# Conditioning in four column groups, norms three steps later, gate rows and y loaded ahead, merged tokens split as they are merged

## The chip, the cores and the metric

One core of one Trainium2 chip. The metric is device time in microseconds (us). Engines are named as the profile names them: PE (TensorE matmul), PEld (its weight loads), DVE (VectorE), ACT (ScalarE), POOL (GpSimd), SP (SyncE, which issues all the DMAs named here).

## The reference

One layer over 1024 sample tokens (a 16x64 grid) and 128 prompt tokens, together NT = 1152 columns, with D = 1024:

```
shift, scale, gate = split(silu(cond) @ w_ada + b_ada, 3)
h = rmsnorm(x, norm_g) * (1 + scale) + shift
q, k, v, z_a, u_b, z_b, u_c, z_c, g_a, g_b, g_c = split(h @ w_in)
q, k = rmsnorm per head (64 wide) of q, k
y_a = neighbourhood attention (8 x 16 window, bias) + cached context keys
y_b = Fourier mixing of u_b;  y_c = pooling of u_c
merged = sum over i of sigmoid(g_i) * ((silu(z_i) * y_i) @ p_i)
out = x + gate * (merged @ w_o);   new k and v of the prompt are returned
```

## The kernel before

Nearly every large product is three matmuls of high and low halves (hi·hi, lo·hi, hi·lo; `mm3`, L143 to L146), in fp16 up to the gates and in a rounded fp32 form in the last projection. The program is written in one order; a list scheduler then fixes, before the run, the order of each engine's instructions, and each engine runs its own list strictly in order. A wait at the head of an engine's list therefore holds all that is behind it. [...]

**Conditioning** (0 to 63 us). SP loads 16 pieces of 512 KB of `w_ada` (`wa`, six buffers) and nine tiles of x (`xt`, six buffers). `ada_piece` (L355) multiplies the silu of the two conditioning rows, two columns wide, with a piece in fp32: two matmuls of 512 columns a piece, each recorded twice in the trace (64 records). `ada_end` (L364) copies a finished bank (ACT, `ar`), transposes it on PE and adds the bias on DVE. Meanwhile `xnorms` (L324) squares three tiles of x on ACT, takes the root on POOL and scales on DVE; `x_groups` (L341) transposes them on PE and copies them back by ACT (L350). `h_full` (L407) applies scale and shift, `scale_h` (L380) bounds h, `make_h` (L414) makes its halves. The weight of head pair 0 is squared (L74, `wjk_q`), scaled and split (L98, `wh_q`; L99, `wl_q`).

**Head pairs** (63 to 400 us). A pair's q, k, v come as nine token tiles of 8 steps of `mm3` (`p1_tiles`, L284). `p1_evac` (L247) squares on ACT, sums on DVE, and takes the root and the row of factors on POOL (`rs` L255, `rg` L257). `p1_norm` (L267) multiplies the PSUM tile by `rg` on DVE (`tk`, L271) and splits it into halves (`tok`, L279); it stands after step k == 3 of the next tile. `group_q` (L565) and `group_k` (L581) transpose four normed tiles on PE; `new_pair` makes the pair's factors (`grow`, L232). `chain()` (L757) lays these on steps with `at_(step, ...)`, and 312 steps of it are dealt out between the items of attention (scores, exp, transposes `pt` -> `pts` L686, products `po` L702), after a first fill of 32 + 9 steps.

**Branches and gate rows** (400 to 535 us). Pooling (C) and Fourier (B), then 16 groups of `p_products` (`pec`, `peb` written to DRAM). After every second one a 512 KB piece of the gate weight is loaded (`wg`, L1126 to L1154) and added up on DVE (`acc`, L1144, L1146); four matmuls (`gb`, L1151) sum it over partitions at the end.

**Attention's gates** (535 to 640 us). For four blocks, y is loaded (`ya`, L1195), the product z_a is made (`za`), gated, and multiplied with p_a (`ppa`, L1248).

**Gates by Strassen's method** (640 to 889 us; `xa`, `xb`, `xc`). A finished block of the merged tokens (`mg`) is written to DRAM (`m_d`).

**Output projection** (889 to 998 us). `wo_unit` (L1382) loads and splits w_o, `m_load` and `m_split` (L1399) read the merged tokens back and split them (`mh` L1400, `ml` L1401); 18 tiles of 8 steps of `mm3` (`wo`).

## Time and profile before

| | us |
|---|---|
| three runs | 993.22, 998.97, 997.37 (median 997.37) |
| the profiled execution, its own time | 999.48 |
| its span in the trace | 997.7 |
| busy on POOL, with its share of the span | 228.5 (23%) |
| busy on ACT | 495.0 (50%) |

The span is 1.8 us short of the execution's own time. Times below are counted from the start of the span. An engine's busy share is an average over the stages just named; what a stage costs is read from what waits last in it. In lists of waits, the engine that waited stands first and behind the arrow what it waited for.

### The profile page before, as it was taken

The page shows a single profiled execution, that of the slowest core. Times are in us where ns is not written, and L with a number is a line of the kernel's source. Part 1 is how long each engine was busy: PE and PEld are TensorE (multiplying, and loading weights), DVE is VectorE, ACT ScalarE, POOL GpSimd, SP SyncE. Part 2 cuts the span into 40 slices and gives each one's busy share as a digit, 9 for nine tenths or more (in the row PEclk, how much of TensorE's full clock was granted, in tenths as well). Part 3 has the DMA queues.
Part 4 walks back from the last instruction along what each step waited for, and adds up shares of the span by engine and source line. Part 5 has one row for each costly group of instructions (what it writes and reads, how often), then busy time and mean ns, then how long its engine had stood idle before and what let it go on. Part 6 is the DMA issues. An engine that isn't in the chain of part 4 may idle for free.

```text
span 997.7 us, 17549 instructions
## 1 busy us (share of the span) xinstructions
PE 916.2 (92%) x6510; PEld 675.4 (68%) x6510; DVE 648.5 (65%) x1431; ACT 495.0 (50%) x1023; POOL 228.5 (23%) x373
## 2 busy tenths in 40 slices
PE   4976799898889999989989899999999999989998
PEld 1333466565656676657975479888888888868886
DVE  1365557667676664797543559878979788766422
ACT  4683557557556665545435434555554544433100
POOL 1056454444545320041100320002021020200000
PEclk9978989999999999999999999999999999989999
DMA  7743322312302322411878502443435332248421
GB/s 305 272 133 104 101 70 78 81 40 75 83 25 75 101 74 78 145 53 49 257 245 281 173 33 91 173 139 112 145 118 163 98 115 95 68 142 303 130 95 54
DMA packets 72038, 123.95 MB, mean 124 GB/s; under 512 B 10592, under 2 KB 39180, under 8 KB 71953
## 3 DMA queue, kind: packets, MB, share of 16 engines
q1 hardware_dynamic: 71953, 122.84, 38.6%
q8 instruction: 51, 0.84, 0.3%
q14 instruction: 34, 0.28, 0.1%
HBM read 87.41 MB, written 28.84 MB: 117 GB/s over the span
## 4 chain that ended last, share of the span: by engine, by line
PE 65%; DVE 11%; DMA 8%; POOL 7%; ACT 5%; issue 3%; SPq 1%; ACTq 0%; DVEq 0%; POOLq 0%
PE wo L144 3%; PE wo L145 3%; PE wo L146 3%; PE xc L146 3%; PE xb L144 3%; PE xb L146 3%; PE xb L145 3%; PE xc L144 3%; PE xc L145 3%; POOL rs L255 3%; PE xa L144 3%; PE xa L146 3%; PE xa L145 3%; PE ppa L144 2%; PE ppa L146 2%
## 5 line engine op out<-in xcount | busy, mean ns | idle before, releaser
L145 PE MATMUL p<-wl_q,hh 128*128 128x384 f16 x288 | 96.9, 336 | 1.0 <-DVE wl_q L99 1.0
L144 PE MATMUL p<-wh_q,hh 128*128 128x384 f16 x288 | 96.1, 337 | 0.0
L146 PE MATMUL p<-wh_q,hl 128*128 128x384 f16 x288 | 96.0, 336 | 0.0
L673 ACT ACTIVATE sn<-sn,mn 128x512 f32<-128x512 f32 x64 | 46.3, 724 | 30.6 <-DVE mn L662 29.1
L144 PE MATMUL wo<-woh,mh 128*128 128x512 f32 x144 | 57.6, 400 | 3.0 <-ACT mh L1400 3.0
L145 PE MATMUL wo<-wol,mh 128*128 128x512 f32 x144 | 56.9, 397 | 0.0
L146 PE MATMUL wo<-woh,ml 128*128 128x512 f32 x144 | 56.5, 394 | 0.0
L686 DVE TENSOR_TENSOR pts<-pt,pts 128x512 f16<-128x512 f32 (+1 forms) x72 | 46.0, 639 | 11.3 <-ACT pts L685 10.9
L88 POOL TENSOR_SCALAR wsc_g<-wsc_g 128x1 f32<-128x1 f32 x12 | 2.7, 228 | 207.0 <-DVE wsc_g L87 207.0
L271 DVE TENSOR_TENSOR tk<-p,rg 128x256 f32<-128x256 f32 x36 | 15.3, 424 | 52.6 <-POOL rg L257 52.6
L1441 DVE TENSOR_TENSOR yo<-wo,gb 128x512 f32<-128x512 f32 x18 | 12.4, 690 | 53.7 <-PE wo L146 53.7
L662 DVE CUSTOM_DVE_ANT_0 sn<-s,bias 128x512 f32<-128x512 f32 x64 | 43.6, 681 | 5.4 <-PE s L658 5.4
L702 PEld LDWEIGHTS <-pts 128*128 128x128 f16 x792 | 33.6, 98 | 16.0 <-DVE pts L686 9.2
L145 PEld LDWEIGHTS <-wh_m 128*128 128x128 f16 x288 | 28.4, 98 | 23.1 <-issue 6.5
L146 PEld LDWEIGHTS <-hl 128*128 128x128 f16 x288 | 29.0, 101 | 21.2 <-issue 3.6
L146 PEld LDWEIGHTS <-wl_m 128*128 128x128 f16 x288 | 28.4, 99 | 21.3 <-DVE wl_m L99 2.5
L702 PE MATMUL po<-vw,pts 128*128 128x64 f16 x576 | 32.6, 193 | 11.0 <-DVE pts L686 7.0
L144 PEld LDWEIGHTS <-wh_m 128*128 128x128 f16 x288 | 28.8, 100 | 18.5 <-issue 1.7
L145 PEld LDWEIGHTS <-hh 128*128 128x128 f16 x288 | 29.0, 101 | 17.8 <-issue 1.9
L144 PEld LDWEIGHTS <-hh 128*128 128x128 f16 x288 | 29.0, 101 | 17.4 <-issue 1.4
L362 PE MATMUL pa<-wa,sil 128*2 128x512 f32 x64 | 31.0, 633 | 10.1 <-DMA wa<-in_wss_dram 10.1
L685 ACT CAST pts<-pt 128x512 f16<-128x512 f32 (+1 forms) x72 | 38.9, 540 | 1.3 <-PE pt L683 1.2
(654 smaller groups left out, 3060.4 us busy)
## 6 DMA issues: line engine op xcount, KB each, us to landing
wa<-in_wss_dram SPq DMA_DIRECT2D x16, 512.0 KB, 4.3
wr_q<-in_w_dram SPq DMA_DIRECT2D x16, 384.0 KB, 3.0
wr_m<-in_w_dram SPq DMA_DIRECT2D x24, 256.0 KB, 3.0
pp_c<-pec SPq DMA_DIRECT2D x24, 192.0 KB, 2.7
pp_b<-peb SPq DMA_DIRECT2D x24, 192.0 KB
pp_a<-pea SPq DMA_DIRECT2D x24, 192.0 KB, 1.8
ppxc<-pp_c SPq DMA_DIRECT2D x16, 288.0 KB, 2.7
ppxb<-pp_b SPq DMA_DIRECT2D x16, 288.0 KB, 2.9
```

The costliest lines, as they stand in the source:

```text
L144: T.matmul(out, lh, rh, start=first, stop=False)
L145: T.matmul(out, lh, rl, start=False, stop=False)
L146: T.matmul(out, ll, rh, start=False, stop=last)
L255: G.tensor_tensor(rs, rs, mhalf, op=ALU.pow)
L271: V.tensor_tensor(tk, pt[:, :256], rg.rearrange("p g d -> p (g d)"), op=ALU.mult)
L362: T.matmul(pa[:2], sil[:, k], wa[i][:, q], start=(k == 0), stop=(k == KT - 1))
L662: V.tensor_tensor_reduce(out=sn, in0=pS, in1=bt.rearrange("p a b -> p (a b)"), op0=ALU.add, op1=ALU.min, scale=1.0, scalar=3e38, accum_out=mn)
L673: S.activation(e[:, :n], it["sn"], AF.Exp, bias=it["mn"], scale=-1.0, accum_out=sm_)
L685: S.copy(pts[:, 0, :n], pt[:, :n])
L686: V.tensor_tensor(pts[:, 1, :n], pt[:, :n], pts[:, 0, :n], op=ALU.subtract)
L702: T.matmul(po[:, :64], it["pts"][:, a, j * P:(j + 1) * P], it["vl"][j][:, c_ * 64:(c_ + 1) * 64], start=(j == 0 and i == 0), stop=(j == nk ...
L1441: V.tensor_tensor(yo, pt, gb[0 if t == 8 else 1][:, cols], op=ALU.mult)
```

## The change

It has five parts. (a) The silu rows are padded to 32 columns and these matmuls go to four column groups of PE (`tile_position`); the groups are summed by a matmul with `pick` in place of the transposes. Two `wa` pieces are loaded ahead of x, and the weight of pair 0 is squared, scaled and split ahead of the last `ada_end`. (b) Five small operations of `new_pair` go from POOL to DVE. (c) `p1_norm` stands after k == 6, and `group_q`, `group_k`, `setup_prompt` and `windows` later accordingly; the fill is 32 + 13. (d) Weights of the products and gate rows are loaded two ahead, `acc` is spread over the groups, the four `gb` stand in the last two groups, and two of the four `ya` loads stand before the end of the products. (e) Columns 0 to 511 of the merged tokens are split as they are merged and stay in SBUF (`mh0`, `ml0`); only the rest goes through `m_d`. The first three `wo_unit` stand in the last Strassen unit.

```diff
...
-    sil = pers.tile([P, KT, 2], F32, name="sil")
+    sil = pers.tile([P, KT, 32], F32, name="sil")
+    pick = pers.tile([P, 2], F32, name="pick")
...
-                    G.tensor_scalar(gs4[:, 2 * i:2 * i + 2], sc_[:, 2 * p:2 * p + 2], inv, None, op0=ALU.mult)
-                    G.tensor_tensor(g[:, 2 * i:2 * i + 2], row.unsqueeze(1).to_broadcast([P, 2, 64]),
+                    V.tensor_scalar(gs4[:, 2 * i:2 * i + 2], sc_[:, 2 * p:2 * p + 2], inv, None, op0=ALU.mult)
+                    V.tensor_tensor(g[:, 2 * i:2 * i + 2], row.unsqueeze(1).to_broadcast([P, 2, 64]),
...
-                G.tensor_scalar(i8, inv, 0.125, None, op0=ALU.mult)
+                V.tensor_scalar(i8, inv, 0.125, None, op0=ALU.mult)
...
-                        if k == 3 and late:
+                        if k == 6 and late:
...
-                V.tensor_tensor(sil.rearrange("p k c -> p c k"), ex.rearrange("p (c k) -> p c k", c=2),
+                G.memset(sil, 0.0)
+                V.tensor_tensor(sil[:, :, 0:2].rearrange("p k c -> p c k"), ex.rearrange("p (c k) -> p c k", c=2),
                                 col[:, 0:16].rearrange("p (c k) -> p c k", c=2), op=ALU.mult)
+                V.reduce_sum(pick, ident.rearrange("p (g c) -> p c g", g=4)[:, 0:2], axis=AX.X)
...
-                        T.matmul(pa[:2], sil[:, k], wa[i][:, q], start=(k == 0), stop=(k == KT - 1))
+                        g = 32 * (k % 4)
+                        T.matmul(pa[g:g + 32], sil[:, k], wa[i][:, q], start=(k < 4), stop=(k >= 4), tile_position=(0, g))
                 def ada_end(b):
-                    ar = st.tile([2, 512], F32, tag="ar", name=f"ar{b}", bufs=2)
-                    S.copy(ar, pas[b][:2, :])
+                    ar = st.tile([P, 512], F32, tag="ar", name=f"ar{b}", bufs=1)
+                    S.copy(ar, pas[b])
...
                     for j in range(4):
-                        T.transpose(pb[:, 2 * j:2 * j + 2], ar[:, j * P:(j + 1) * P], ident[:2, :2])
+                        T.matmul(pb[:, 2 * j:2 * j + 2], ar[:, j * P:(j + 1) * P], pick, start=True, stop=True)
...
-                for what in (0, 1, 2, "w0", "w1", 3, 4, 5, "w2", "w3", "w4", "w5"):
+                for what in ("w0", "w1", 0, 1, 2, "w2", "w3", 3, 4, 5, "w4", "w5"):
...
+                    if i + 6 < 16:
+                        if i == 6:
+                            run(prep0, 1)
+                        load_wa(i + 6)
...
-                    while nwa < 16 and nwa - 6 <= i:
-                        load_wa(nwa)
-                        nwa += 1
...
-                    if i == 8:
+                    if i == 7:
...
-                    if i == 9:
-                        run(prep0, 1)
...
-                    if i == 13:
-                        run(prep0, 1)
+                        wu0 = run(prep0, 6)
...
-                            at_(4, group_q, c, 0)
-                            at_(6, group_k, c, 0)
-                            at_(14, setup_prompt, c)
+                            at_(11, group_q, c, 0)
+                            at_(14, group_k, c, 0)
+                            at_(20, setup_prompt, c)
...
-                            at_(14, setup_prompt, c)
+                            at_(20, setup_prompt, c)
...
-                            at_(46, group_q, c, 0)
-                            at_(50, group_k, c, 0)
+                            at_(52, group_q, c, 0)
+                            at_(55, group_k, c, 0)
...
-                            at_(3, lambda: p1_norm(*late.pop()))
+                            at_(6, lambda: p1_norm(*late.pop()))
...
-                            at_(2, windows, b)
-                            at_(5, group_q, b, 1)
-                            at_(7, group_k, b, 1)
+                            at_(4, windows, b)
+                            at_(12, group_q, b, 1)
+                            at_(15, group_k, b, 1)
...
-                fill(32 + 9)
+                fill(32 + 13)
                 LEAD = 16
...
+            ya = yctx.enter_context(tc.tile_pool(name="ya", bufs=1, **TW))
+            yas = {}
+            def ya_load(i):
+                yas[i] = ya.tile([P, NT], F32, tag="y", name=f"ya{i}", bufs=2)
+                nc.sync.dma_start(yas[i], yT_d[i])
...
-                for m in range(8):
-                    for br, ks, c0 in (("c", (2, 3), 6), ("b", (0, 1), 4)):
-                        u = load_unit(pw[m][:, c0 * P:(c0 + 2) * P], 256, f"p{br}{m}")
-                        p_products(br, m, [(u, 0), (u, P)], ks, gp, 4)
-                    if m == 7:
-                        m_load(9)
-                    wg = gp.tile([P, D], F32, tag="wg", name=f"wg{m}", bufs=2)
-                    nc.sync.dma_start(wg, wgate[m])
+                wgs = {}
+                def load_wg(m):
+                    wgs[m] = gp.tile([P, D], F32, tag="wg", name=f"wg{m}", bufs=3)
+                    nc.sync.dma_start(wgs[m], wgate[m])
+                def add_wg(m):
...
+                def gate_rows(c, n):
+                    a = slice(n * 512, (n + 1) * 512)
+                    pt = bank("po", f"gb{c}{n}")
+                    T.matmul(pt, ones, acc[c][:, a], start=True, stop=True)
+                    gr = gp.tile([1, 512], F32, tag="gr", name=f"gr{c}{n}", bufs=1)
+                    V.tensor_tensor(gr, pt[0:1, :], brow[:, a], op=ALU.add)
+                    nc.sync.dma_start(g_d[c:c + 1, a], gr)
...
+                load_pu(0)
+                load_pu(1)
+                load_wg(0)
+                load_wg(1)
+                for j in range(16):
+                    m, i = divmod(j, 2)
+                    br, ks = (("c", (2, 3)), ("b", (0, 1)))[i]
+                    if j + 2 < 16:
+                        load_pu(j + 2)
+                    u = pus.pop(j)
+                    if i == 0 and m + 2 < 8:
+                        load_wg(m + 2)
+                    p_products(br, m, [(u, 0), (u, P)], ks, gp, 4)
+                    if j < 14 and j % 2 == 1:
+                        add_wg(j // 2)
+                    if j == 12:
+                        add_wg(7)
+                    if j == 13:
+                        ya_load(0)
+                    if j >= 14:
+                        for n in range(2):
+                            gate_rows(j - 14, n)
+                    if j == 14:
+                        ya_load(1)
+                        m_load(9)
...
             t_tiles(tp, range(4), "a")
-            with tc.tile_pool(name="ya", bufs=1, **TW) as ya:
+            if True:
                 for i in range(4):
-                    y = ya.tile([P, NT], F32, tag="y", name=f"ya{i}", bufs=2)
-                    nc.sync.dma_start(y, yT_d[i])
+                    y = yas[i]
+                    if i in (1, 2):
+                        ya_load(i + 1)
...
         m_d = dr.tile([8, P, NT], F32, name="m_d")
+        fe = ctx.enter_context(tc.tile_pool(name="fe", bufs=1, **TW))
+        TB = (0, 512, 1152)
+        mh, ml = [fe.tile([P, KT, 512], F32R, name="mh0"), None], [fe.tile([P, KT, 512], F32R, name="ml0"), None]
...
+        def m_split(m, c, src, a, d):
+            S.copy(mh[c][:, m, d], src[:, a])
+            V.tensor_tensor(ml[c][:, m, d], src[:, a], mh[c][:, m, d].bitcast(F32), op=ALU.subtract)
...
                 if bi == 2:
-                    nc.sync.dma_start(m_d[m][:, a], mg)
+                    if j == 0:
+                        m_split(m, 0, mg, slice(0, 512), slice(0, 512))
+                        nc.sync.dma_start(m_d[m][:, 512:HN], mg[:, 512:HN])
+                    else:
+                        nc.sync.dma_start(m_d[m][:, a], mg)
...
+                if n == len(units) - 1 and i in (2, 3, 4):
+                    wo_unit(0, i - 2, fe, 3)
...
-        wo_ = {}
...
-        wo_unit(0, 0)
...
+        mh[1] = fo.tile([P, KT, NT - 512], F32R, name="mh1")
+        ml[1] = fo.tile([P, KT, NT - 512], F32R, name="ml1")
...
-        def m_load(m, j):
+        def m_load(m):
+            parts = []
...
-                src = gx.tile([P, HN], F32, tag="pp", name=f"mr{m}{j}", bufs=4)
-                nc.sync.dma_start(src, m_d[m][:, j * HN:(j + 1) * HN])
+                src = gx.tile([P, HN + 64], F32, tag="mr", name=f"mr{m}", bufs=2)
+                nc.sync.dma_start(src, m_d[m][:, 512:NT])
+                m_split(m, 1, src, slice(0, HN + 64), slice(0, HN + 64))
...
-                src = last_m[m - 6, j]
-            if j == 0:
-                m_split(m, 0, src, slice(0, 512), slice(0, 512))
-                m_split(m, 1, src, slice(512, HN), slice(0, HN - 512))
-            else:
-                m_split(m, 1, src, slice(0, HN), slice(HN - 512, NT - 512))
-        for k in range(8):
-            if k > 0:
-                wo_unit(0, k)
-            m_load(k, 0)
+                m_split(m, 1, last_m[m - 6, 0], slice(512, HN), slice(0, HN - 512))
+                m_split(m, 1, last_m[m - 6, 1], slice(0, HN), slice(HN - 512, NT - 512))
+        for k in range(3, 8):
+            wo_unit(0, k, fo, 8)
...
```

ACT's list, before, where the last bank of the conditioning (`ar3`) is copied; `wjk_q` are the squares of pair 0's weight:

```order
L74 ACTIVATE wjk_q00_409,wss_q0_408<-wr_q00_368 128x768
L74 ACTIVATE wjk_q01_411,wss_q0_408<-wr_q01_370 128x768
L74 ACTIVATE wjk_q02_413,wss_q0_408<-wr_q02_372 128x768
L74 ACTIVATE wjk_q03_415,wss_q0_408<-wr_q03_374 128x768
L366 COPY ar3_421<-pa3_403 2x512
L74 ACTIVATE wjk_q10_861,wss_q1_860<-wr_q10_761 128x768
L410 ACTIVATE xT_116<-xT_116,sh_85,gs_84 128x1024
L410 ACTIVATE xT_116<-xT_116,sh_85,gs_84 128x128
L74 ACTIVATE wjk_q11_863,wss_q1_860<-wr_q11_763 128x768
L416 ACTIVATE hh0_94<-xT_116,shs_77 128x1152
L98 ACTIVATE wh_q00_462<-wr_q00_368,wsc_q0_455 128x768
L98 ACTIVATE wh_q01_466<-wr_q01_370,wsc_q0_455 128x768
```

ACT's list after, at the same place:

```order
L74 ACTIVATE wjk_q00_407,wss_q0_406<-wr_q00_293 128x768
L74 ACTIVATE wjk_q01_409,wss_q0_406<-wr_q01_295 128x768
L74 ACTIVATE wjk_q02_411,wss_q0_406<-wr_q02_297 128x768
L74 ACTIVATE wjk_q03_413,wss_q0_406<-wr_q03_299 128x768
L98 ACTIVATE wh_q00_422<-wr_q00_293,wsc_q0_417 128x768
L98 ACTIVATE wh_q01_426<-wr_q01_295,wsc_q0_417 128x768
L98 ACTIVATE wh_q02_430<-wr_q02_297,wsc_q0_417 128x768
L98 ACTIVATE wh_q03_434<-wr_q03_299,wsc_q0_417 128x768
L370 COPY ar3_447<-pa3_438 128x512
L74 ACTIVATE wjk_q10_841,wss_q1_840<-wr_q10_764 128x768
```

The four halves `wh_q` have moved from behind the last `ar`, and behind the first `hh`, to ahead of both.

PE's list before, where the transposes of `group_q` of pair 0 (`pq0_0`) begin; `p1_0_8` is the tile of the prompt:

```order
L146 MATMUL p1_0_8_769<-wh_q02_470,hl1_97 128x384
L572 LDWEIGHTS tok0_0_665
L572 MATMUL pq0_0_807<-id16_71,tok0_0_665 128x2x4x16
L572 LDWEIGHTS tok0_1_687
L572 MATMUL pq0_0_807<-id16_71,tok0_1_687 128x2x4x16
```

PE's list after, at the same place; all 24 matmuls of `p1_0_8` and 12 of the next tile, `p1_0_5`, now stand ahead of it, where it was 15 of `p1_0_8`:

```order
L146 MATMUL p1_0_5_833<-wh_q01_426,hl0_96 128x384
L573 LDWEIGHTS tok0_0_668
L573 MATMUL pq0_0_855<-id16_71,tok0_0_668 128x2x4x16
L573 LDWEIGHTS tok0_1_690
L573 MATMUL pq0_0_855<-id16_71,tok0_1_690 128x2x4x16
```

PE's list before, right behind the last Strassen matmul; `wo0_t` is output tile t, `woh0k` and `wol0k` the halves of w_o of step k:

```order
L144 MATMUL wo0_0_11571<-woh00_11469,mh0_11477 128x512
L145 MATMUL wo0_0_11571<-wol00_11470,mh0_11477 128x512
L144 MATMUL wo0_1_11618<-woh00_11469,mh0_11477 128x512
L145 MATMUL wo0_1_11618<-wol00_11470,mh0_11477 128x512
L144 MATMUL wo0_2_11661<-woh00_11469,mh0_11477 128x512
L145 MATMUL wo0_2_11661<-wol00_11470,mh0_11477 128x512
```

PE's list after, at the same place:

```order
L144 MATMUL wo0_0_11549<-woh00_11337,mh0_8306 128x512
L145 MATMUL wo0_0_11549<-wol00_11338,mh0_8306 128x512
L146 MATMUL wo0_0_11549<-woh00_11337,ml0_8307 128x512
L144 MATMUL wo0_0_11549<-woh01_11382,mh0_8306 128x512
L145 MATMUL wo0_0_11549<-wol01_11383,mh0_8306 128x512
L146 MATMUL wo0_0_11549<-woh01_11382,ml0_8307 128x512
```

Before, four tiles take step 0 in turn, the products with `mh0` ahead of those with `ml0`; after, tile 0 takes step 0 whole and goes on to step 1.

More of the change, by code (lines that the diff above doesn't have):

```diff
@@ L489, in mixer_layer @@
                 hm = scale_h()
-                wu = run(prep0, 5)
+                wu = wu0
+                inverse_of(wu["sc"])
                 c0 = None
@@ L1147, in mixer_layer @@
[L1147 to L1154 removed]
+                            V.scalar_tensor_tensor(acc[c], wgs[m], sil[:, m, c:c + 1], acc[c], op0=ALU.mult, op1=ALU.add)
```

53 lines of the change are left out of this document (21 added, 32 removed).

## The prediction

> **What bounds the kernel now.** I read the engine shares first, then a table of stretches of time (us, then busy time of PE, PEld, DVE, ACT, POOL with instruction counts, PE's granted clock, DMA share, GB/s), then the list of PE's waits.
>
> ```profile
> PE 916.2 (92%) x6510; PEld 675.4 (68%) x6510; DVE 648.5 (65%) x1431; ACT 495.0 (50%) x1023; POOL 228.5 (23%) x373
> ...
> 0.00:60.00 60.00, 42.20 (x158) 15.22 (x158) 16.40 (x49) 34.92 (x68) 4.36 (x15) 0.99 0.75 269
> 76.00:130.00 54.00, 38.03 (x226) 22.71 (x225) 27.79 (x85) 25.08 (x57) 28.30 (x47) 0.85 0.38 104
> 130.00:400.00 270.00, 249.76 (x2284) 170.37 (x2282) 176.24 (x536) 169.44 (x422) 112.98 (x224) 0.99 0.26 71
> 475.00:505.00 30.00, 30.00 (x175) 30.00 (x174) 17.54 (x28) 13.99 (x30) 1.72 (x3) 1.00 0.85 274
> 505.00:535.00 30.00, 23.36 (x122) 19.50 (x121) 11.40 (x17) 11.28 (x26) 0.00 (x0) 1.00 0.80 262
> 535.00:560.00 25.00, 20.27 (x125) 12.18 (x124) 11.72 (x27) 13.79 (x28) 3.82 (x8) 1.00 0.74 253
> 640.00:889.00 249.00, 248.56 (x2038) 198.83 (x2038) 201.73 (x319) 117.60 (x179) 33.99 (x38) 1.00 0.38 122
> 889.00:910.00 21.00, 18.02 (x69) 14.43 (x67) 17.80 (x35) 14.59 (x32) 0.00 (x0) 0.84 0.84 275
> ```
>
> PE is busy 92% and idle 81.5 us (997.7 - 916.2). The change takes no large product away, so its gain can only be idle time, half-clock time and PE's part of the conditioning. The stretches show where that lies: 17.8 us of idle in the first 60, 16.0 in 76 to 130 with the clock at 0.85, 20.2 in the attention, 6.6 and 4.7 in 505 to 560, 3.0 at the start of the projection. The Strassen stage has 0.4: nothing is to be won there, only lost.
>
> ```profile
> PE pq L572 <- DVE tok L279: 19.5, 8, 5.9
> PE pa L362 <- DMA wa<-in_wss_dram: 10.1, 1, 10.1
> PE po L702 <- DVE pts L686: 7.5, 10, 1.9
> PE za L144 <- DVE sga L856: 4.7, 2, 3.2
> PE ppc L144 <- DVE oh_pc L64: 4.3, 2, 2.7
> PE pbd L388 <- DVE ab L386: 3.0, 1, 3.0
> ...
> PE gb L1151 <- ACT peb L1123: 2.3, 1, 2.3
> ...
> PE pqp L603 <- DVE tok L279: 2.0, 2, 1.1
> ```
>
> Columns: total us, times, the longest. The normed tokens (`tok`) are the largest: 19.5 + 2.0.
>
> **(a) Conditioning.** From the first `wa` to the last, PE is nearly always busy; the question is what binds once its matmuls overlap.
>
> ```profile
> 8.95 1.06 ACT L329 ACTIVATE xsq<-xt 128x1024 bf16<-128x1024 f32 x1 [6.94 <-DMA xt<-in_xs_dram]
> ...
> 10.28 1.06 ACT L329 ACTIVATE xsq<-xt 128x1024 bf16<-128x1024 f32 x1 [0.19 <-DMA xt<-in_xs_dram]
> ...
> 22.37 1.13 ACT L329 ACTIVATE xsq<-xt 128x1024 bf16<-128x1024 f32 x1
> ...
> 27.40 1.63 ACT L350 COPY xT<-xt 128x384 f32<-128x384 f32 x4 [1.62 <-PE xt L349]
> ...
> 42.28 3.20 ACT L410 ACTIVATE xT<-xT,sh,gs 128x1024 f32<-128x1024 f32 x4
> ...
> 53.18 0.84 ACT L74 ACTIVATE wjk_q<-wr_q 128x768 bf16<-128x768 f32 x1
> ...
> 54.14 0.57 ACT L366 COPY ar<-pa 2x512 f32<-2x512 f32 x1
> ```
> ```profile
> L362 PE MATMUL pa<-wa,sil 128*2 128x512 f32 x64 | 31.0, 633 | 10.1 <-DMA wa<-in_wss_dram 10.1
> ...
> 59.68 0.59 PE L85 MATMUL pw_q<-wss_q,onesp 128*128 128x4 f32 x2
> ...
> 61.93 0.14 DVE L95 RECIPROCAL wsc_q<-wsc_q 128x1 f32<-128x1 f32 x1
> ...
> 62.94 1.48 PE L144 MATMUL p<-wh_q,hh 128*128 128x384 f16 x4
> ```
>
> The last bank is copied (`ar`) by 54.7, and the first product of the pairs starts at 62.94, 8.2 later; all later work hangs on it. By the order printed above, ACT's list becomes the bound. x lands in pieces of 512 KB, the second 1.33 behind the first (8.95, 10.28). Two pieces of `wa` now precede x: the first square starts at 11.6. A square with its readout takes some 1.17 (the 0.84 of a `wjk` has a pitch of 0.96): three end at 15.1. Root, scaling and the first transposes take 3.8, as from the end of square 5 (23.6) to 27.40: copies from 18.9, eight at 0.41, to 22.2. Squares 3 to 5, of which only the last stood behind these copies, now all do: 25.7, and so on: 3.8 and eight copies, 32.8; three squares and an `ar` (0.57), 36.9; 3.8 and eight copies, 44.0; three pairs of `h_full` at 1.6 and an `ar`, 49.4; four `wjk`, 53.2; the scale of the weight, 59.68 to 62.07 here, 2.4: 55.6; four `wh_q`, taken at the 0.84 of a `wjk` of that size, 59.0; the last `ar`, 59.6. That is 4.9 later than 54.7. Behind it the same 8.2, and some 0.3 each for the small operations new on DVE and for the matmul with `pick`: **+5.5; I take +6** with the waits of copies for PE that the sum leaves out. The waits of `h_full`'s copies shown (1.62 in one row, three groups a round) make that 5 at most: +11. If ACT's queue costs nothing, DMA and the tail bind: 16 pieces of `wa`, nine of x and four weights of 384 KB are 28 pieces of 512 KB; 8.95 + 27 x 1.33 = 44.9, and 1.0 for the last matmul and `ar`, 8.2 behind it: 54.1, -9. So -9 to +11.
>
> [...]
>
> **(b), (c) First pair and attention.**
>
> ```profile
> 94.92 0.29 PE L572 MATMUL pq<-id,tok 128*128 128x128 f16 x1 [5.85 <-DVE tok L279]
> 97.29 0.29 PE L572 MATMUL pq<-id,tok 128*128 128x128 f16 x1 [2.08 <-DVE tok L279]
> ...
> L271 DVE TENSOR_TENSOR tk<-p,rg 128x256 f32<-128x256 f32 x36 | 15.3, 424 | 52.6 <-POOL rg L257 52.6
> ...
> 79.60 7.24 DMA gt<-in_rpbp_dram
> ...
> L255 POOL TENSOR_TENSOR rs<-rs,mhalf 128x4 f32<-128x4 f32 x10 | 11.4, 1139 | 0.7
> L232 POOL TENSOR_TENSOR grow<-qgb,gs 128x128 f32<-128x128 f32 x2 | 13.9, 6930 | 0.2
> ```
>
> DVE stands 52.6 us at `tk`, waiting for POOL, 1.46 a tile; that holds `pts` and `tok`, and so PE. Three steps later a `tk` is asked for when its `rg` is there. In the first pair 141 products stand ahead of the last transpose of `pq0_0` now and 156 then; POOL's chain is the same, with bias work that needs `gt` (landed at 86.8, 23.9 behind the first product) in its list ahead of tile 0's root. By that chain the four `tok` are ready at 23.9, four roots of 1.14 with some 0.9 for the two small POOL operations beside each, 32.1, and 0.42 each for `tk` and `tok`: 33 behind the first product. PE has done its 156 by 29.5: 0.17 a product, from 0.23 at 512 columns in the fence under (e), and 3 more, as the first 6 us run at half clock (4 in 1.48). That leaves 3.5; the bias work itself adds to POOL's list, and I take it that of the 7.9 us **5 stay**. `grow` (13.9 on POOL, one of the two nearly all of it) goes to DVE at some 0.4; it ended before the first squares, so I cost it at nothing; without that cover it would be 13. Of the 16.0 idle in 76 to 130, I take back 16.0 less 5 and 1.5 for other small waits, 9.5; the clock of 0.85 over 54 us is 8.1 lost, of which 3.5 go with the gaps before it: **-13** (-16 to -8).
>
> In the attention the rest of the `tok` waits goes (21.5 less 7.9 and 5.9 is 7.7, of which I count 5.5 behind 130), and few of the 7.5 at `pts`, which wait for ACT too: **-5** (-10 to +6, rival 5's wait at a part of the tiles). The later `group_q`, `group_k` and the fill of 13 steps move instructions, add none, and queue nothing new on SP or POOL.
>
> **(d) 475 to 560.**
>
> ```profile
> L1146 DVE SCALAR_TENSOR_TENSOR acc<-wg,sil,acc 128x1024 f32<-128x1024 f32 x14 | 17.3, 1280 | 18.4 <-DMA wg<-in_wgate_dram 18.4
> ```
>
> DVE waits 18.4 us at `acc` for `wg`; behind it stand the splits (`oh_pc`) that PE waits for (4.3), and the four `gb` (2.3) and `za` (4.7) wait for loads asked for late. Loads two ahead remove these 11.3 and 1.7 of half clock. But the DMA carries the same bytes: 30 x 0.85 + 30 x 0.80 + 25 x 0.74 = 68.0 us of full use in 85. With 13 us less its share would be 0.94, while 0.85 is what was seen with PE never waiting. At 9 less it is 0.89: **-9** (-13 to -4). On SP's list two `ya` loads now stand ahead of `m_load(9)`, whose weights nobody needs before the gates of the last blocks.
>
> **(e) 640 to the end.**
>
> ```profile
> 892.24 0.80 PE L144 MATMUL wo<-woh,mh 128*128 128x512 f32 x1 [2.98 <-ACT mh L1400]
> ...
> 897.95 0.59 PE L146 MATMUL wo<-woh,ml 128*128 128x512 f32 x1
> 898.38 0.39 PE L144 MATMUL wo<-woh,mh 128*128 128x512 f32 x1
> ...
> 910.65 0.39 PE L145 MATMUL wo<-wol,mh 128*128 128x512 f32 x1
> 910.88 0.39 PE L146 MATMUL wo<-woh,ml 128*128 128x512 f32 x1
> ```
>
> PE waits 2.98, then runs to 898.4 at half clock (0.43 from start to start, against 0.23 at the end of the fence). With `mh0`, `ml0` and three `wo_unit` ready, it goes on at once: 2.98, some 3.3 of half clock (0.20 by 16 products in 6.1 us), and 2.7 of the later waits for `mr` and the splits: 9.0, less 1 for `woh03` and on, whose loads and splits still come late: **-8** (-9 to -4). The price is 8 casts and 8 subtractions of 512 columns in the Strassen stage (some 0.7 each, an estimate from the 0.84 of a `wjk` at 768), where DVE is busy 201.7 of 249 and PE never waits; its 47 idle us hide the 6. Without that cover it is +6.
>
> **Sum:** +6 - 13 - 5 - 9 - 8 = -29. Against the profiled execution, 999.48, that is **970**; the median of the runs shown is 2.1 lower.
>
> **Rivals.**
> 1. *The conditioning is bound by DMA*: ACT's order costs nothing as squares find slack in waits. For it: ACT is busy 34.92 of 60 only. Against it: the last `ar` stands behind the four `wjk` and four `wh_q`, and these behind `h_full`. 970 - 15 = 955; chance 0.14.
> 2. *PE still binds the conditioning*, column groups not overlapping; then `pa` keeps its 31.0 us, and ACT's later squares come on top: some +6 more, 976; chance 0.12. [...]
> 3. *The 475 to 560 stage keeps its length*, DMA-bound at 0.80: +8, 978. For it: 274 GB/s is reached with PE never waiting; chance 0.12.
> 4. *The waits at `tok` only move*: POOL's chain, not the place of `tk`, sets `tok`, and PE waits at `pq` as long: +16, 986; chance 0.08.
> 5. *Slower.* `tk` reads PSUM, so tile t's bank is free only after it; tile t + 2 needs the bank one step behind k == 6, where there were four. 312 - 72 = 240 steps in 270 us are 1.1 us each: 1.1 of room for a `tk` of 0.42. Against it: six steps behind its tile, `tk` has had 7 us for a chain that POOL does in some 3. From 1.1 us of wait at each of 27 tiles on, the gain is gone; with DVE's 1.46 turned whole into PE waits at every tile, 39 us: 1009; chance 0.04.
>
> **The numbers.** My forecast has 0.46; several rivals at once, 0.04. The likeliest alone lies at 962 to 978; the range that leaves out less than 2 in 10 is 953 to 986: it holds the forecast, rivals 1 to 3 and, at its edge, rival 4 (0.92). Faster than 0.5% (which a measurement of this kernel can tell from no change) 0.92, within it 0.04 (the several rivals at once), slower 0.04.
>
> **What will show it.** The first product of the pairs at 66 to 71, with ACT's last `ar` at 58 to 62 and ACT idle little ahead of it (rival 1 has it near 46; under rival 2 the `pa` records keep their spacing); one wait of about 5 us at `pq0_0` and none at `pq0_1`; `tk` waiting for `rg` under 10 us in all, no PE wait at the first product of a tile (rival 5); 475 to 560 shorter by 9 with a DMA share near 0.9; `wo` starting within 0.5 us of the last `xa` at full clock. Wrong by much would be a POOL or SP list that now holds up something I cost at nothing.

## The result, and the profile after

The changed kernel took **1007.32 us** (median of 4 runs, 1006.43 to 1008.62) where the kernel before took 997.50 beside it (4 runs, 993.22 to 998.97): ratio **1.0105**, 95% interval 1.0077 to 1.0133. It is slower by about 1%; the prediction said 970, 953 to 986. The profiled execution took 1007.29, its span 1005.5, 7.8 longer than before.

To see where this comes from, the span is cut at points that both kernels have: the first or last matmul of a kind in each trace (`p` the pair products, `s` the scores, `u` the last attention step's merge product, `ppc`/`ppb` and `za` the branches in 475 to 560, `xc` the last Strassen unit, `wo` the projection). All in us:

| stage | before | after | difference | forecast |
|---|---|---|---|---|
| start to first `p` | 62.94 | 76.30 | **+13.4** | +6 |
| to first `s` | 67.19 | 65.81 | -1.4 | -13 |
| to last `u` (attention) | 267.61 | 271.84 | **+4.2** | -5 |
| to first `ppc` | 74.91 | 76.46 | +1.6 | 0 |
| to last `ppb` | 55.19 | 59.89 | +4.7 | -9 with the next |
| to last `za` | 60.13 | 48.93 | **-11.2** | |
| to first `xc` | 52.10 | 51.41 | -0.7 | 0 |
| to first `wo` | 252.16 | 248.92 | -3.2 | -8 with the next |
| to last `wo` | 101.08 | 101.46 | +0.4 | |

Each stage is read from one trace of each kernel. The later experiments show how far kernels that leave a stage alone differ in it: by 1 to 2 us in the first three stages, by 2.6 in the fourth, but by 4.0 from first `ppc` to last `ppb` and by 5.3 from there to last `za`. Of the nine kernels without (d), the trace of before is the longest over these two stages: 115.3, where the other eight have 110.7 to 112.9.

Every term of the sum missed by 2 us or more. (d) brought -6.5 by the table (108.8 - 115.3 from first `ppc` to last `za`), or -3.0 against the middle of those eight, 111.8; (e) brought -2.8; the first pair and the attention together brought +2.8 where -18 was forecast, and the conditioning cost more than twice its price. The page of after, first the busy time of each engine, then the group of `tk`:

```profile
PE 913.6 (91%) x6526; PEld 676.4 (67%) x6526; DVE 651.4 (65%) x1446; ACT 490.6 (49%) x1017; POOL 207.0 (21%) x354
...
L272 DVE TENSOR_TENSOR tk<-p,rg 128x256 f32<-128x256 f32 x36 | 15.2, 424 | 53.6 <-POOL rg L258 53.6
```

PE's idle time grew from 81.5 to 91.9 us (1005.5 - 913.6) while its busy time fell by 2.6 only. And DVE stands at `tk` for **53.6** us where it was 52.6: the wait that part (c) is about is all there. The stretches, in the columns of the first fence of the prediction:

```profile
0.00:60.00 60.00, 34.18 (x155) 15.41 (x155) 12.33 (x35) 29.84 (x59) 4.62 (x16) 0.89 0.72 268
60.00:76.00 16.00, 5.92 (x22) 3.62 (x22) 9.37 (x32) 12.09 (x22) 1.24 (x5) 0.50 0.29 100
...
505.00:535.00 30.00, 28.62 (x156) 28.62 (x157) 15.75 (x24) 14.35 (x30) 0.00 (x0) 0.94 0.93 305
535.00:560.00 25.00, 24.69 (x134) 18.98 (x133) 11.63 (x22) 12.61 (x29) 0.79 (x2) 1.00 0.89 298
```

PE was busy 42.20 of the first 60 us before and is 34.18 now: its conditioning matmuls did get shorter. Yet the first product comes at 76.3, after 16 us in which PE does little and has half its clock. The windows of 505 to 560 have little idle time and a DMA share near 0.9, as forecast; but all work there comes some 18 us later than before, and a wait of 4.07 us at `ppb` lies across their start, from 502.3 to 506.4 (under (d) below). PE's list of waits, after (total, times, longest):

```profile
PE po L703 <- DVE pts L687: 13.7, 15, 3.0
PE xt L352 <- DVE xt L336: 7.8, 2, 5.5
PE pb L373 <- ACT ar L370: 6.4, 3, 3.5
PE pq L573 <- DVE tok L280: 6.1, 3, 3.0
...
PE p L144 <- DVE tk L272: 4.9, 1, 4.9
...
PE pt L684 <- DVE pts L687: 3.2, 4, 1.1
...
PE pk L588 <- DVE tk L272: 2.1, 1, 2.1
...
PE wo L144 <- ACT woh L1319: 1.1, 1, 1.1
```

`tok` fell from 21.5 to 6.1, but `pts` rose from 7.5 to 13.7 + 3.2, and PE waits for `tk` itself, 4.9 + 2.1: **the waits moved**. In the conditioning, waits for DVE and ACT have grown: 7.8 at `xt` (0.2 before) and 6.4 for `ar` (0.7 before).

### The profile page after: what moved, and what is told of

Read it like the earlier page. It is cut to its first block, busy times and chain, and to the rows that moved or that the text cites. A ratio compares the mean times of both kernels' runs of the same rounds, so it can differ in the third digit from the quotient of the medians.

```text
span 1005.5 us, 17517 instructions
## 1 busy us (share of the span) xinstructions
PE 913.6 (91%) x6526; PEld 676.4 (67%) x6526; DVE 651.4 (65%) x1446; ACT 490.6 (49%) x1017; POOL 207.0 (21%) x354
## 4 chain that ended last, share of the span: by engine, by line
PE 62%; DVE 13%; POOL 8%; DMA 6%; ACT 6%; issue 3%; SPq 2%; ACTq 0%; DVEq 0%; POOLq 0%
PE wo L144 3%; PE wo L146 3%; PE wo L145 3%; POOL rs L256 3%; PE xc L146 3%; PE xb L144 3%; PE xb L145 3%; PE xb L146 3%; PE xc L144 3%; PE xc L145 3%; PE xa L144 3%; PE xa L146 3%; PE xa L145 3%; POOL rg L258 2%; PE ppa L144 2%
## 5 line engine op out<-in xcount | busy, mean ns | idle before, releaser
L272 DVE TENSOR_TENSOR tk<-p,rg 128x256 f32<-128x256 f32 x36 | 15.2, 424 | 53.6 <-POOL rg L258 53.6
L703 PE MATMUL po<-vw,pts 128*128 128x64 f16 x576 | 33.1, 193 | 17.4 <-DVE pts L687 13.3
L279 ACT CAST tok<-tk 128x256 f16<-128x256 f32 x36 | 14.6, 405 | 60.1 <-DVE tk L272 60.0
L684 PE MATMUL pt<-ident,sn 128*128 128x128 f32 x256 | 38.8, 274 | 3.7 <-DVE pts L687 3.2
```

Of the source, the lines that this page charges most:

```text
L272: V.tensor_tensor(tk, pt[:, :256], rg.rearrange("p g d -> p (g d)"), op=ALU.mult)
L279: S.copy(t16[:, :, 0], tkv)
L684: T.transpose(pt[:, j * P:(j + 1) * P], it["e"][:, j * P:(j + 1) * P], ident)
L703: T.matmul(po[:, :64], it["pts"][:, a, j * P:(j + 1) * P], it["vl"][j][:, c_ * 64:(c_ + 1) * 64], start=(j == 0 and i == 0), stop=(j == nk ...
```

## Experiments: one part at a time

Each experiment is compared with the kernel before, run on the same chip beside it; "first product" and the stages are the marks of the table above, read from the profiled execution of each, so from one trace, with the scatter given there; the ratios have intervals.

**Part (a) alone**: all of the diff's conditioning edits, nothing else.

> Part (a) alone on the kernel before. Theory S (each part costs what its stage shows in the two traces): first product of the pairs near 76 instead of 62.9, and nothing given back later: +12 to +14 us. The prediction's term was +6. Theory I (the parts disturb each other): the same +13 in the first 76 us, but up to 5 us given back in the first pair, as loads of the pair are then early: +8.

1008.17 us, ratio 1.0092 (1.0065 to 1.0118); first product at 76.11, first to last attention mark 268.03. Part (a) by itself costs as much as the whole change.

**Parts (b) and (c) alone**: `grow` on DVE, `k == 6` and the later `at_` numbers.

> Parts (b) and (c) alone on the kernel before. Theory S: tk still stands some four to eight places behind its sum in DVE's list, so it waits for rg as before (52 to 54 us in all); the first pair gains 1 to 2 and the attention up to the pooling loses 4 to 6: +3 to +5 us. The prediction's terms were -13 and -5: -18. Theory I: with the clock and the loads of the conditioning as before, the first pair gains most of its waits: -8 to -12.

1000.87, ratio 1.0022 (1.0003 to 1.0042); attention 272.03 against 267.61 before, and DVE waits 52.3 at `tk`. The part meant to remove that wait leaves it and lengthens the attention.

**Part (d) alone**: loads of the gate rows, `ya` and the `p` units ahead.

> Part (d) alone. Theory S and the prediction agree nearly: -7 by the traces (472.7 to 640.1 before, 490.4 to 650.6 after), -9 by the prediction. Theory I: less than -4, if the stage profits from the loads being late elsewhere.

989.62, ratio 0.9903 (0.9874 to 0.9932), so -9.3; `ppc` to `ppb` 55.32, on to `za` 48.93.

**Part (e) alone**: merged tokens split in the Strassen stage, `wo` started ahead.

> Part (e) alone. Theory S: -3 us, all of it the wait of 3.0 ahead of the first wo; the time from the first wo to the end stays at 101. The prediction's term: -8.

992.81, ratio 0.9952 (0.9930 to 0.9974), -6.1; `xc` to first `wo` 248.92, -3.2.

**Parts (d) and (e) together.**

> Parts (d) and (e) on the kernel before. If they add up: -9.3 - 6.1 = -15 us. If (e) slows the products of C and B when (d) stands before them (that stage took 59.9 us with all parts, 55.3 with (d) alone, 58.1 with (e) alone): -10 to -12.

987.09, ratio 0.9896 (0.9872 to 0.9920): -10.0, not the -15.4 of the two alone. By the ratios, which set each kernel against before on its own chip, the two alone make 0.9855, 4.1 us less than 0.9896; the three intervals (half-widths 2.9, 2.2 and 2.4 us) leave about 4.4 put together, an estimate, so that the parts disturb each other is not clear of noise. In its trace `ppc` to `ppb` is 58.88 where (d) alone has 55.32; what that is, is under (d) below.

## Experiments: the conditioning

Part (a) is two things: column groups (the hunks with `sil` of 32, `tile_position` and `pick`), and an order (two `wa` ahead of x, the weight of pair 0 squared and split after piece 11). They can be run apart.

```diff
 # groups alone: order of before, and
+T.matmul(pa[g:g + 32], sil[:, k], wa[i][:, q], start=(k < 4), stop=(k >= 4), tile_position=(0, g))
...
 # order alone: matmuls of before, and
+for what in ("w0", "w1", 0, 1, 2, "w2", "w3", 3, 4, 5, "w4", "w5"):
...
+if i == 11: wu0 = run(prep0, 6)
```

> Of part (a) only the column groups and the sums by pick, with loads, squares and weight split in the order of before. Theory O (the order of ACT's list and of the loads makes the loss): PE's matmuls shrink by some 20 us and the chain over ACT, POOL, DVE and PE becomes the bound: first product at 58 to 62, -1 to -5 us. Theory G (the grouped matmuls make the loss, as PE falls idle and to half clock): first product at 68 to 72, +5 to +9.

> Of part (a) only the new order: wa ahead of x, third group of x at piece 7, pair 0's weight squared, scaled and split ahead of the last bank; matmuls two columns wide and transposes as before. Theory O: first product at 72 or later, +9 or more. Theory G: first product at 64 to 66, +1 to +3.

Groups alone: 1002.97, ratio 1.0051 (1.0036 to 1.0066), first product at 68.83. Order alone: 997.38, 1.0010 (0.9988 to 1.0032), 63.87. So +5.9 and +0.9, and +13.2 together: the order costs almost nothing as long as PE's matmuls are the bound, and 7 once they are not.

**Late split**: part (a) with the squares of the weight after piece 13, and its scale and split after the first `scale_h`.

```diff
-wu0 = run(prep0, 6)
+if i == 13: run(prep0, 1)
...
-wu = wu0; inverse_of(wu["sc"])
+wu = wu0 = run(prep0, 5)
```

> Part (a) alone, but pair 0's weight squared after piece 13 and scaled and split behind scale_h as before; groups and order of loads as in (a). In the trace of part (a) alone 61.0 to 66.5, the scale and the four wh_q, stand ahead of the last bank's copy. Theory O with the split as its main term: first product at 68 to 70, +2 to +4. Theory O with the loads and the squares of x as its main term, or theory G: first product at 73 or later, +7 or more.

1003.01, ratio 1.0055 (1.0034 to 1.0077), first product at 70.16, 6.0 ahead of part (a). The early split was one of the costs.

**Wide matmuls without groups**: `sil` padded to 128 columns, the wide `ar` and `pick`, everything else as before. ACT's list is then that of before, row for row.

```diff
-sil = pers.tile([P, KT, 2], F32, name="sil")
+sil = pers.tile([P, KT, P], F32, name="sil")
-T.matmul(pa[:2], sil[:, k], wa[i][:, q], start=(k == 0), stop=(k == KT - 1))
+T.matmul(pa, sil[:, k], wa[i][:, q], start=(k == 0), stop=(k == KT - 1))
```

> The matmuls of the conditioning 128 columns wide (silu rows padded to 128), ungrouped, with the wide copy ar and the sums by pick as in the change; ACT's list is then that of before, row for row. If the groups' shorter time on PE, and the list that follows from it, make the loss of 5.9 us seen with the groups alone: first product at 62 to 64.5, -1 to +1 us. If the wide copy or pick make it: 67 or later, +4 to +6.

998.79, ratio 1.0009 (0.9995 to 1.0024), first product at 63.80. So the wide bank, its copy and `pick` are not the cost.

**x ahead of everything**: groups, (d) and (e), with eight x tiles loaded first (five `wa` buffers).

> Parts (d), (e) and the column groups, with eight tiles of x loaded ahead of all wa (eight buffers of x, five of wa), all squares of x early, pair 0's weight loaded ahead of the last five pieces. If the chain of squares, copies and transposes bound the grouped conditioning, it now ends early and DMA binds: first product at 52 to 58, -15 to -20 us with (d) and (e) (-10 of their own). If idle and half clock on PE bind: first product at 62 or later, -10 or less.

996.75, ratio 0.9991 (0.9975 to 1.0007), first product at 67.64: no way out. Several things differ at once in this kernel (ACT's list among them), so it does not say which of them is late.

**Groups with ACT's list of before**: the groups alone, with two dependencies that keep ACT's order at two places: squares 3 and 4 ahead of the first copies, and the `hh` from the second on behind the last `wh_q`.

```diff
+with tc.issue_after(xsquares(XG[1], (0, 1)).ins):
     run(xg, 8)
+xnorms(XG[1], (2,))
...
+with tc.issue_after(whq) if k else ExitStack():
     make_h(k)
```

> The column groups alone, with two squares of the second group of x issued on ACT ahead of the copies of the first, and hh 1 and on behind the last wh_q, as in ACT's list of before. If the altered list makes the 5.9 us: first product at 62 to 65, -1 to +2 us. If PE itself makes it (idle, half clock, and single grouped matmuls that stand between transposes): 67 or later, +4 to +6.

993.60, ratio **0.9954** (0.9931 to 0.9977), first product at 63.15, against 68.83. The only difference to the groups alone is the order, so the **order of ACT's list is what made the groups slow**, and the groups by themselves are no loss. ACT's timeline in this kernel (start, length, engine, line, operation, in brackets the idle time before it and whom it waited for):

```profile
16.78 1.06 ACT L336 ACTIVATE xsq<-xt 128x1024 bf16<-128x1024 f32 x1
...
17.84 3.12 ACT L363 COPY xT<-xt 128x384 f32<-128x384 f32 x8
...
27.59 3.16 ACT L363 COPY xT<-xt 128x384 f32<-128x384 f32 x8 [5.11 <-PE xt L362]
...
41.47 1.76 ACT L363 COPY xT<-xt 128x384 f32<-128x384 f32 x4 [6.87 <-PE xt L362]
...
50.87 0.59 ACT L380 COPY ar<-pa 128x512 f32<-128x512 f32 x1
```

Squares 3 and 4 fill time before the first copies, where the groups alone wait 4.80; the two later waits stay, at 5.1 and 6.9 (7.4 and 6.9 there). The last `ar` ends at 51.5, with the groups alone at 57.1, and from there to the first product both take 11.7 (8.2 before). So what the order saved lies at the squares, and the place of `hh` has no effect on the first product. That product comes no earlier than before (62.94): the 4.5 us by which this kernel is faster lie mostly in the stage behind it, 63.59 from first `p` to first `s` against 67.19, and no run shows why. The same engine in the changed kernel:

```profile
13.21 1.06 ACT L332 ACTIVATE xsq<-xt 128x1024 bf16<-128x1024 f32 x1
...
21.33 3.16 ACT L353 COPY xT<-xt 128x384 f32<-128x384 f32 x8 [1.31 <-PE xt L352]
...
26.73 1.06 ACT L332 ACTIVATE xsq<-xt 128x1024 bf16<-128x1024 f32 x1
...
34.26 1.63 ACT L353 COPY xT<-xt 128x384 f32<-128x384 f32 x4 [6.39 <-PE xt L352]
...
41.27 1.06 ACT L332 ACTIVATE xsq<-xt 128x1024 bf16<-128x1024 f32 x1
...
48.87 2.01 ACT L353 COPY xT<-xt 128x384 f32<-128x384 f32 x5 [6.45 <-PE xt L352]
...
63.19 3.41 ACT L98 ACTIVATE wh_q<-wr_q,wsc_q 128x768 f16<-128x768 f32 x4 [2.04 <-DVE wsc_q L79]
66.50 0.56 ACT L370 COPY ar<-pa 128x512 f32<-128x512 f32 x1
```

Here the last `ar` ends at 67.1. The squares of a group stand behind the copies of the group before, so ACT does nothing for 6.4 us behind the sixth square and the ninth (its readout ends at 27.88 and 42.42), and the last `ar` stands behind the whole weight. What PE does in that gap, in the changed kernel:

```profile
30.00 1.97 PE L352 MATMUL xt<-ident,xt 128*128 128x128 f32 x8 [5.45 <-DVE xt L336]
31.90 1.92 PE L366 MATMUL pa<-wa,sil 128*32 128x512 f32 x2
33.75 1.12 PE L352 MATMUL xt<-ident,xt 128*128 128x128 f32 x4
```

Before, such transposes ran so:

```profile
18.81 2.84 PE L349 MATMUL xt<-ident,xt 128*128 128x128 f32 x24
```

Having waited 5.45 us, PE runs the transposes at half clock (8 in 1.97, with a granted clock of 0.50 from 29.4 to 36.2; before, 24 took 2.84 at 1.00), and two `pa` records between them take 1.92. The copies wait for the last transpose of their tiles.

## Experiments: `tk` and the pair stages

DVE's own list shows why (c) did nothing. From `ss` to `tk` of one tile of the attention, after the change:

```
L253 TENSOR_REDUCE ss1_3_1504<-sq1_3_1502 128x4
L261 SCALAR_TENSOR_TENSOR v161_1042<-p1_1_3_1397,...
L705 TENSOR_SCALAR yt0_0_0_1416<-po0_1_0_0_1535,...
L676 RECIPROCAL ri0_0_0_2_1585<-sm0_0_0_2_1583 128x1
L272 TENSOR_TENSOR tk1_3_1615<-p1_1_3_1397,rg1_3_1509 128x256
```

Between the two stand three instructions, as before the change. Over the tiles `tk` follows `ss` by 4.2 places before and 4.1 after. The program asks for `p1_norm` three steps later, but the scheduler that makes DVE's list puts `tk` where it was, and DVE stands there until POOL has `rg`. So I made the list obey: a dependency puts `tk` behind the newest second half of `pts` (no data pass, only order). With (c), (d) and (e), without (a) and (b):

```diff
+lastv[:] = [V.tensor_tensor(pts[:, 1, :n], pt[:, :n], pts[:, 0, :n], op=ALU.subtract)]
...
+with tc.issue_after(lastv[0].ins) if lastv else ExitStack():
     V.tensor_tensor(tk, pt[:, :256], rg.rearrange("p g d -> p (g d)"), op=ALU.mult)
```

> Parts (c), (d) and (e), with each tk issued on DVE behind the newest pts of attention: on DVE's list it now stands 8.9 places behind its sum on average, where it was 4.2 before and 4.1 after the change. Theory T (tk's place in DVE's list is what makes DVE wait for rg, and the change did not move it): DVE's wait for rg falls from 53 to under 30 us, and the stretch from the first s to the last u from 267.6 (272 with (c)) to 258 to 264: -14 to -20 us in all. Rival (POOL's chain or PSUM banks only move the wait): that stretch stays at 267 or more, -5 to -10 in all.

**972.44**, ratio **0.9744** (0.9712 to 0.9776). `tk` now follows `ss` by 8.9 places on the mean. The attention takes 255.96, 11.7 under before. DVE's waits, this kernel:

```profile
DVE pts L688 <- ACT pts L687: 20.9, 38, 2.8
DVE tk L272 <- POOL rg L257: 17.0, 9, 3.5
```

DVE waits 17.0 at `tk` instead of 53.6, and PE's waits in the attention fell too, to 4.2 us for `pts`:

```profile
PE po L704 <- DVE pts L688: 4.2, 4, 1.8
...
PE p L144 <- DVE tk L272: 1.4, 3, 1.0
```

The same dependency in the **whole change**, with (a):

> The whole change with each tk issued on DVE behind the newest pts. If tk's place is what parts (b) and (c) lacked: the stretch from the first s to the last u falls from 271.8 to 255 to 258, 988 to 993 us, below the kernel before. If the late and half-clocked conditioning of part (a) spoils it: 998 or more.

990.82, ratio 0.9925 (0.9902 to 0.9949): attention 256.72, DVE's wait at `tk` 15.4, first product still at 75.74. One dependency turns +9.8 into -7.2. This kernel has (b) and the one above has not, and their attention is the same to 0.8 us; (b) was never run apart from (c).

**Forced, but with the steps of before** (`k == 3`, the old `at_` numbers): is the later step needed at all?

> Parts (d) and (e) with tk forced behind the newest pts, but the norm at k == 3 and all steps as before; tk then stands 5.5 places behind its sum on average, and 8.9 with the later step. If only the place on DVE's list counts: the wait for rg at 35 to 45 us, the stretch from the first s to the last u 262 to 266, 981 to 985 us. If the later step by itself is needed on PE (pq too early): 985 to 988, as (d) and (e).

980.04, ratio 0.9810 (0.9785 to 0.9834): attention 259.36, DVE waits 33.1 at `tk`, PE 14.3 at `pq`. So the dependency alone brings 8.0 beyond (d) and (e) by the medians (-18.0 against -10.0), and the later steps 7.1 more (-25.2). Here `tk` stands 5.5 places behind `ss`, not 8.9, so the runs do not tell whether these 7.1 come from the place on DVE's list or from a program that asks for `tok` later.

**First pair forced too**: there no `pts` exists yet, so `tk` is put behind the next tile's evacuation.

```diff
+late.append(evac)
+if len(late) > 1: p1_norm(*late.pop(0))
```

> As e11, and in the first pair each tk behind the evacuation of the next tile. If the first pair's waits at pq (4.9) have the same cause as in the attention: they fall under 2 us, and from the first product to the first s takes 62 to 64 instead of 65.6, -2 to -3 us against e11. If POOL's chain binds there: no change within 1 us of e11.

971.53, ratio **0.9727** (0.9706 to 0.9748), the fastest run of all, but no different from 972.44. First `p` to first `s` is 64.48, `pq` still waits. PE's waits in that stretch:

```profile
PE p L144 <- DVE tk L274: 6.1, 1, 6.1
PE pq L577 <- DVE tok L282: 5.8, 2, 3.1
```

In no kernel did this stage fall below 63.5. POOL's timeline there shows what is left:

```profile
90.61 0.23 POOL L254 TENSOR_SCALAR rs<-ss 128x4 f32<-128x4 f32 x1
90.92 0.89 POOL L637 TENSOR_TENSOR bias<-mk,gt 128x384 f32<-128x384 bf16 x1
91.76 1.22 POOL L255 TENSOR_TENSOR rs<-rs,mhalf 128x4 f32<-128x4 f32 x1
93.06 0.61 POOL L257 TENSOR_TENSOR rg<-grow,rs 128x256 f32<-128x256 f32 x1
93.75 0.23 POOL L254 TENSOR_SCALAR rs<-ss 128x4 f32<-128x4 f32 x1
94.06 1.02 POOL L255 TENSOR_TENSOR rs<-rs,mhalf 128x4 f32<-128x4 f32 x1
95.17 0.61 POOL L257 TENSOR_TENSOR rg<-grow,rs 128x256 f32<-128x256 f32 x1
```

POOL has no pause in these rows; the fourth `rg`, counted from a first one at 84.92, ends at 95.8, 33.3 behind the first product at 62.47. `tk` waits for that wherever it stands. No run shortened POOL's chain, so that it is the bound of this stage rests on these rows alone.

## Experiments: the loads of 475 to 560

**Gate-row loads spread** over the units instead of two ahead, with (d) and (e):

```diff
+wg_load = {1: 0, 3: 1, 5: 2, 7: 3, 9: 4, 10: 5, 11: 6, 12: 7}
+wg_add = {3: 0, 5: 1, 7: 2, 9: 3, 11: 4, 12: 5, 13: 6, 14: 7}
```

> Parts (d) and (e) with the gate weights' loads spread over the 16 groups instead of two ahead at the start. In the traces with (d) a peb waits 2.4 to 4.1 us for its buffer while the DMA share is 0.98 or more, and PE's clock is 0.66 behind it in (d) and (e) together. If these early loads make that wait: no wait over 1 us in the products of C and B, that stretch 54 to 55.5 us instead of 58.9, -13 to -15 us in all. If not: -10 as (d) and (e) together.

987.06, ratio 0.9894 (0.9873 to 0.9915), the same as 987.09 with two ahead. `ppc` to `ppb` is 56.11 with one wait of 2.4 in another place. Moving these loads changed nothing that the medians show.

**Both mended**: (c), (d), (e), groups with ACT's order kept, `tk` forced, without (b).

> Parts (c), (d), (e), the column groups with ACT's order kept, and tk forced. If the two mends add up (-25.6 of e11 and -4.5 of e13): first product at 62 to 64, the first s 63 to 64 later, 966 to 970 us. If the groups take back what tk's place gives, or the other way: 972 or more.

973.15, ratio 0.9755 (0.9720 to 0.9791). First product at 61.67, attention 255.59; but `ppc` to `ppb` is 59.70, by a wait of 3.87 for `peb` and the half clock behind it:

```profile
473.00:483.00 10.00, 10.00 (x51) 10.00 (x50) 8.12 (x12) 4.71 (x10) 0.00 (x0) 0.84 0.98 335
```

Against the kernel with `tk` forced, 3.1 us are gained ahead of this place (1.2, 1.6 and 0.4 in the first three stages), and 4.2 are given back at it. The first are no more than the scatter of single traces; the medians, 973.15 and 972.44, do not differ. So the two mends do not add up: -24.6 by the medians, -29.6 the two alone.

**Weight of pair 0 loaded still earlier**, ahead of the last five `wa`, squares at piece 11, on the kernel above:

> As e17, with pair 0's weight loaded ahead of the last five pieces of wa and squared earlier; still scaled and split behind scale_h. If the weight binds the start of the pairs now: first product at 57 to 60, 2 to 4 us under e17. If the chain behind the last ar binds: first product within 1 us of e17's, and the same time.

978.79, ratio 0.9820 (0.9789 to 0.9850), slower than the kernel above; neither thing expected came. First product at 65.10, 3.4 later; PE waits 4.42 for an `ar` at 49.95.

## Why the prediction was wrong, step by step

**(c), the step that failed.** The prediction says: "Three steps later a `tk` is asked for when its `rg` is there." It is not: the lists show `tk` 4.1 places behind `ss`, and DVE waits 53.6. I had compared PE's list before and after, and the instruction that waits is on DVE's. What did move is PE's use of `tok` (`group_q`, `group_k` later), so the waits at `tok` went, while DVE, held at `tk` just as long, delivered `pts` later: 13.7 + 3.2 instead of 7.5. The attention alone, before and then after, each from its first `s` to its last `u`:

```profile
130.10:397.70 267.60, 247.36 (x2269) 169.00 (x2268) 176.24 (x536) 168.76 (x421) 112.88 (x224) 0.99 0.25 69
```
```profile
142.10:414.00 271.90, 247.07 (x2268) 167.97 (x2266) 176.95 (x544) 169.00 (x420) 107.73 (x211) 0.99 0.24 68
```

and with `tk` forced:

```profile
128.40:384.40 256.00, 244.40 (x2268) 167.53 (x2266) 180.09 (x535) 168.20 (x420) 111.80 (x221) 0.99 0.27 73
```

PE's work is the same to 3 us in all three; idle is 20.2, 24.8 and 11.6. The mechanism of (c) was therefore right, and worth 12 us in the attention where I had 5, if it is made to happen. That it did not happen is the rival I left out: that the change doesn't do what it says.

**First pair, -13 forecast, -1.4.** POOL's chain came as forecast (33 behind the first product), and 6.1 us stayed at `pq` where I had 5. But "1.5 for other small waits" was too little: 2.1 at `pk` and 4.9 at a product that waits for a bank still read by `tk` are new. Idle in this stretch went from 17.0 to 13.1, not to 6.5, and as gaps stayed, so did the half clock (a mean of 0.84, 0.83 before): PE's busy time rose by 2.4. The bank (the kernel keeps two under `p1`, L53) is rival 5's mechanism, at one tile; with `tk` forced late at every tile it cost 1.4 us in the attention. That POOL's chain moves the waits instead of ending them is rival 4, and its chance of 0.08 was too low.

**(a), +6 forecast, +13.4.** The kind was right: ACT's list becomes the bound, and the groups do overlap (rival 2 is out; rows below). The mis-sized term is the step from a square to the copies, taken at 3.8 each time from a row of before. Measured, from the end of a readout to the copies: 7.0 (14.4 to 21.33), 6.4 and 6.45. The three excesses, 3.2, 2.6 and 2.6, make 8.4; the first square came 1.0 earlier than the sum had it (10.60 against 11.6), and the last `ar` 7.5 later than its 59.6. In the row of before PE went at full clock (1.00 from 25.8 to 27.5), and 1.6 us passed from the first transpose (25.80) to the copies (27.40); here, behind its wait of 5.45, it ran its transposes at half clock (0.50) with `pa` records between, and 4.3 passed (30.00 to 34.26). I priced ACT's list with PE's durations of a PE-bound stretch. The late split and the kept ACT order show that the list, not the groups, is the cost.

**(d), -9 forecast.** Right alone: -9.3 by the medians, -7.6 in its own stages (104.25 from first `ppc` to last `za`, against the 111.8 of the kernels without it). In the whole change these stages gave -3.0 by the same measure, as `ppc` to `ppb` grew by 4.6 (59.89 against 55.32). PE's timeline of after at that place, and the ten us from there:

```profile
506.38 0.45 PE L144 MATMUL ppb<-th,oh_pb 128*128 128x384 f32 x1 [4.07 <-ACT peb L1125]
```
```profile
500.00:507.00 7.00, 2.93 (x17) 2.62 (x16) 5.42 (x7) 1.11 (x3) 0.00 (x0) 1.00 0.99 339
507.00:517.00 10.00, 10.00 (x50) 10.00 (x50) 8.01 (x12) 4.61 (x10) 0.00 (x0) 0.83 0.95 325
```

The copy of `peb` had itself waited 10.5 us for a buffer whose store had not landed; ACT's timeline:

```profile
505.85 0.94 ACT L1125 COPY peb<-ppb 128x384 f32<-128x384 f32 x2 [10.54 <-DMA pp_c<-pec]
```

The DMA is full (0.99) ahead of it, the limit that the prediction named, though it is a late store and no late load that PE meets; and 1.7 us of clock go behind it. In all five kernels that have both (d) and the column groups this wait is 3.9 to 4.2 us and `ppc` to `ppb` takes 59.5 to 60.1; in the five with (d) and no groups that have this wait, it is 2.4 to 3.3, and the stage takes 55.3 to 58.9. So it is the groups that go with the longer wait, 400 us behind their place; why is open. Two kernels show how much hangs on that clock. Part (d) alone, at this wait, and the ten us around it:

```profile
486.00 0.45 PE L144 MATMUL ppb<-th,oh_pb 128*128 128x384 f32 x1 [2.37 <-ACT peb L1124]
```
```profile
485.00:495.00 10.00, 9.00 (x52) 9.00 (x53) 8.98 (x12) 5.34 (x12) 0.00 (x0) 1.00 1.02 346
```

Parts (d) and (e):

```profile
488.09 0.69 PE L144 MATMUL ppb<-th,oh_pb 128*128 128x384 f32 x1 [2.54 <-ACT peb L1124]
```
```profile
485.00:495.00 10.00, 7.46 (x27) 7.14 (x26) 8.00 (x10) 3.79 (x8) 0.00 (x0) 0.66 0.98 339
487.48:494.30 6.82, 6.21 (x19) 6.21 (x20) 4.82 (x7) 3.79 (x8) 0.00 (x0) 0.50 0.98 331
```

A gap of 2.4 or 2.5 us either way, but a clock of 1.00 and of 0.66 in the ten us: 3.4 of them are lost to the clock in one (0.3 of it while PE still waits) and none in the other. The half clock lasts 6.82 us, where it lasted 3.4 in the changed kernel (507.3 to 510.7). These runs do not show why half clock follows one of the two gaps and not the other; no run here shifted a gap on purpose.

The 3 us of clock make up most of the 3.6 by which these two traces differ from `ppc` to `ppb`. They do not account for the 5.4 by which (d) and (e) together fell short of the two alone: the one profiled execution lies 3.2 above the median of its kernel and the other 2.2 below, and the kernel with spread loads, at the same median of 987.06, takes 56.11 here.

**(e), -8 forecast, -2.8.** The 2.98 at the start went (-3.2 with its neighbours), and it showed alone as -6.1 in the medians (-4.8 in its own stages: -3.2 and -1.6). The term of "2.7 of the later waits" did not hold: before, the projection from first to last `wo` took 101.08, and after 101.46. The clock that was lost there is gained: it is 1.00 throughout, where before 3.1 us went at its start. But a wait of 1.14 for `woh` is new, some products of the first 10 us stand 0.30 to 0.34 apart, and over parts of the rest they stand 0.231 to 0.234 apart where before it was 0.227; together these take about 3 us back. No run shows what spreads them.

**The sum.** The parts alone give +9.3, +2.0, -9.3 and -6.1: -4.1. The whole is +9.8, 13.9 more. Put together from the medians of the parts and the table of stages, 6.1 of these lie in (d) and (e) (-9.3 and -6.1 alone, -6.5 and -2.8 here; the longer wait at `peb` is the piece that the traces name), 5.8 in the stages of (a) to (c) and those between (+17.1 there, +11.3 alone), and 2.0 between the profiled execution and the median. That split is bookkeeping and no finding: it sets medians against two single traces, with a scatter of 4 to 5 us in two of the stages. That the whole is dearer than its parts is clear (the five intervals leave some 5.6 us put together, an estimate); why, beyond the wait at `peb`, stays open.
